# One expert picked from the counts of all but the last tile, its weights asked for ahead of the sort

## The chip, the cores and the metric

The kernel runs on one core of a Trainium2 chip. The metric is the device time of one execution in microseconds; the median of three runs of the kernel before is 2537.41 us.

## The reference, cut to what matters

Two layers, each a token mixer followed by a mixture of experts (MoE). Layer 0 routes 768 tokens (256 context and 512 latent), layer 1 only the 512 latent ones. A router picks a group, and in it the two best of 32 experts for each token; each expert is a gated MLP (1024 to 512 to 1024).

```python
def expert_ffn(xb, e, w_g, w_u, w_d):
    return (jax.nn.silu(xb @ w_g[e]) * (xb @ w_u[e])) @ w_d[e]

def hier_moe(h, w_rg, b_rg, w_re, b_re, w_g, w_u, w_d):
    ...
    flat_e = (grp[:, None] * EXPERTS_PER_GROUP + top_i).reshape(-1).astype(jnp.int32)
    ...
    counts = jnp.zeros((N_EXPERTS,), jnp.int32).at[flat_e].add(1)
    ...
    y = lax.map(lambda a: expert_ffn(a[0], a[1], w_g, w_u, w_d), (xb, blk_e))
    out = jnp.zeros((T + 1, D), F32).at[buf_tok].add(y.reshape(P, D).astype(F32) * buf_w[:, None])
    return out[:T].astype(h.dtype)
```

The weights of an expert are 6 MB (in pieces of 1 MB: four of w_gu, the gate and up matrices together, and two of w_d), and each of the 32 is used in each layer.

## The kernel before

The mixer leaves the tokens as tiles of 128 (six in layer 0, `TL=[0..5]`; four in layer 1, `TL=[2..5]`). A loop over the tiles (L979 to L993) then interleaves the last part of the mixer's output (`mix`) with the router (`norm2`), a generator whose pieces run some rounds later: norm, transposes, router matmuls (L883, result `lgt` on VectorE, L885), the choice of two experts (one-hot rows `OH1`, `OH2`, their sum `M`, L907), positions within an expert (L910 to L912), and the running count `Ms` (L913). The matmuls of this part share one PSUM bank, `ov` (the pool `pso`). At the end of the loop, expert 0's six weight loads are issued.

Behind the loop come loads of the modulation rows `g2` (L1020 to L1027; twelve DMAs in layer 0; nfin and six in layer 1), and the sort (L1084 to L1108): a key of 32 times the count, with a large constant added for the first `NS` experts, whose numbers are known to the program (NS is 1 in layer 0 and 2 in layer 1); a rank from comparisons; and `oi`, the expert number of each rank. The table `SLOTS` gives each rank its number of slots of 32 tokens; what doesn't fit goes to an overflow loop (L1226) that runs as often as is counted in `oi[32]`.

The MoE loop (L1202 to L1218) goes through the ranks: expert 0 (in layer 1, experts 0 and 1), then small and large ranks in turn. For each it reads the expert's number from `oi` into a register of SP (`values_load`, L1203: a TENSOR_LOAD and two short register instructions), issues six loads of 1 MB (`wload`, L959 to L973), gathers the rows of tokens by indirect DMA on GpSimd (L1060), and does the matmuls (L1153 with w_gu, L1178 with w_d). `wload` lets each load wait for the landing of the load four before it. Sixteen buffers of 1 MB are free for weights at the stage's start; the 17th load takes over a buffer of expert 0, once its first products are done.

What sets the order: all these loads, the register loads and the g2 loads are issued by SP, one behind the other, in the order that a scheduler gives when the program is built. Each DMA on SP also waits for the DMA eight before it (eight semaphores in turn). The reload of `br`, the router's bias for layer 1 (L848), is among them: it may overwrite the old one once layer 0's last `lgt` is written.

Of the kernel before, what the change touches and what calls it, by code (L numbers as in the profile page):

```python
# [12 lines left out]
I32 = mybir.dt.int32  # L13
U32 = mybir.dt.uint32
AF = mybir.ActivationFunctionType
OP = mybir.AluOpType
AX = mybir.AxisListType
ET = mybir.EngineType
# [7 lines left out]
NE = 32  # L26
# [1 line left out]
BIG = 4194304.0  # L28
NSL = (1, 2)

SLOTS = ([4, 5, 4, 4, 4] + [3] * 5 + [2] * 18 + [1] * 4, [2, 2] + [3] * 3 + [2] * 11 + [1] * 16)


T1_CA, T1_SA, T1_CR, T1_SR = 0, 512, 1024, 1536
# [27 lines left out]
def tile_backbone(ctx: ExitStack, tc: tile.TileContext, a: dict, out: bass.AP, stop=None, dbg=None):  # L62
    nc = tc.nc
    PE, ACT, DVE, POOL, SP = nc.tensor, nc.scalar, nc.vector, nc.gpsimd, nc.sync
# [19 lines left out]
    def unit(name, dtype=F32, n=2048):  # L84
        return big.tile([128, n], dtype, name=nm(name), tag="c8")
# [16 lines left out]
    def pso():  # L102
        return ps(psov, "ov")

    def small(n, name, dtype=F32, bufs=2):
        return sm.tile([128, n], dtype, name=nm(name), tag=name, bufs=bufs)
# [22 lines left out]
    ident, tri, iota1, iota0, i64 = (cp[:, CP[k][0]:CP[k][1]] for k in ("ident", "tri", "iota1", "iota0", "i64"))  # L129
    tok2, hbm2, zc, bo = (cp[:, CP[k][0]:CP[k][1]] for k in ("tok2", "hbm2", "zc", "bo"))  # L130
# [6 lines left out]
    ones = const(128, "ones")  # L137
# [259 lines left out]
    def layer(l, xt_l, xt_c):  # L397
        full = l == 0
        NS = NSL[l]
        TL = [0, 1, 2, 3, 4, 5] if full else [2, 3, 4, 5]  # L400
# [397 lines left out]
        for bi, b in enumerate("RAF"):  # L798
# [6 lines left out]
            for d in range(8):  # L805
                gp = ahead.pop(0) if ahead else gates(bi, d)
                w = split_load(a["w_br"][l, bi, d]).rearrange("p w (k c) -> p w k c", k=4)
# [45 lines left out]
        Ms = cst.tile([128, NE], F32, name=f"Ms_{l}", tag="Ms_")  # L853
        DVE.memset(Ms, 0.0)

        def norm2(t):
# [29 lines left out]
            g8, gi, gf = small(8, "g8"), small(8, "gi", U32), small(1, "gf")  # L886
# [18 lines left out]
            DVE.tensor_scalar(oh2, iota0, mf[:, 1:2], None, op0=OP.is_equal)  # L905
            M = small(32, "M")
            DVE.tensor_tensor(M, oh1, oh2, op=OP.add)  # L907
            yield
            pp = pso()
            PE.matmul(pp[:, 0:32], tri, M, start=True, stop=False)  # L910
# [19 lines left out]
        def wout(qd):  # L930
            wq = [unit("wqH", R32).rearrange("p (k c) -> p k c", k=8), unit("wqL", R32).rearrange("p (k c) -> p k c", k=8)]
            for k2 in range(4):
                r = raws.tile([128, 512], F32, name=nm("raw"), tag="raw")
                SP.dma_start(r, a["w_out"][l, qd, k2])
                r3 = r.rearrange("p (k c) -> p k c", k=2)
                ks = slice(k2 * 2, k2 * 2 + 2)
                split_to(wq[0][:, ks, :], wq[1][:, ks, :], r3)
            return wq
# [20 lines left out]
        def wload(e, parts=range(6)):  # L959

            res = []
            for j in parts:
                n, j = ("w_gu", j) if j < 4 else ("w_d", j - 4)
                src = a[n][l, e:e + 1] if isinstance(e, int) else a[n][l, bass.ds(e, 1)]
                src = src[0, j // 2] if n == "w_gu" else src[0]
                t = unit(n)
                d = SP.dma_start(t, src[:, (j % 2) * 2048:(j % 2) * 2048 + 2048])
                if len(queue) >= 4:
                    tc.add_manual_dep(d.ins, queue[-4].ins.name, SYNC,
                                      reason="few transfers of weights stand before a gather")  # L970
                queue.append(d)
                res.append(t)
            return res  # L973

        wq2 = [wout(2), wout(3)]
        early = 0
        first = wload(0, range(early))
        g = {}
        for i in range(len(TL) + 2):  # L979
            if i < len(TL):  # L980
                t = TL[i]
                mix(2, wq2[0], t)
                g[i] = norm2(t)
                next(g[i])
                mix(3, wq2[1], t)
                next(g[i])
            if 0 <= i - 1 < len(TL):
                next(g[i - 1])
            if i >= 2:
                next(g[i - 2], None)  # L990
            n = 6 if i == len(TL) - 1 else early
            first += wload(0, range(early, n))
            early = n  # L993
# [4 lines left out]
            return None  # L998


        t0 = TL[0]
        NP = len(TL)
        PR = cst.tile([128, NT, NE], F32, name=f"PR_{l}", tag="wr")
# [5 lines left out]
        oi = cst.tile([128, NE + 8], I32, name=f"oi_{l}", tag="oi_")  # L1009
        xgs = []  # L1010
        for _ in range(3):
            t = hls.tile([128, 2, 512], F32, name=nm("xg"), tag="hl")
            POOL.memset(t, 0.0)
            xgs += [t[:, 0, :], t[:, 1, :]]
        g2u = unit("g2")
        if not full:
            nf = g2u[:, 1024:2048]
            SP.dma_start(nf, bcast_rows(a["nfin"], 1024))
        g2 = {}
        for j, sz in enumerate((64, 32)):  # L1020
            w = sz * 8
# [49 lines left out]
        def prep(r):  # L1071
            n = SLOTS[l][r]
            col = (P1 if r < NS else PR)[:, t0:6, r]
# [7 lines left out]
        scat = []  # L1081


        perm = unit("perm")  # L1084
        pc = pso()
        PE.matmul(pc[0:32, 0:1], Ms, ones[:, 0:1], start=True, stop=True, skip_group_check=True)
        PE.matmul(pc[0:32, 4:36], ones[:, 0:32], Ms, start=True, stop=True, skip_group_check=True)
        kc, kr, gt, rc = perm[0:32, 0:2], perm[0:32, 32:64], perm[0:32, 64:96], perm[0:32, 2:3]
        DVE.tensor_scalar(kc[:, 1:2], tok2[0:32, 0:1], -0.5, 32.0, op0=OP.mult, op1=OP.add)
        DVE.tensor_copy(kr, kcon[0:32, 0, :])  # L1090
        for r in range(NS):
            DVE.tensor_scalar(kr[:, 0:r + 1], kr[:, 0:r + 1], 2.0 ** 20, None, op0=OP.add)
            DVE.tensor_scalar(kc[0:r + 1, 1:2], kc[0:r + 1, 1:2], 2.0 ** 20, None, op0=OP.add)
        DVE.scalar_tensor_tensor(kc[:, 0:1], pc[0:32, 0:1], 32.0, kc[:, 1:2], op0=OP.mult, op1=OP.add)
        DVE.scalar_tensor_tensor(kr, pc[0:32, 4:36], 32.0, kr, op0=OP.mult, op1=OP.add)
        DVE.tensor_scalar(gt, kr, kc[:, 0:1], None, op0=OP.is_gt)
        DVE.tensor_reduce(rc, gt, axis=AX.X, op=OP.add)
        ev, cc = perm[0:32, 3:4], perm[0:32, 4:5]
        DVE.tensor_copy(cc, pc[0:32, 0:1])
        DVE.tensor_scalar(ev, tok2[0:32, 0:1], 0.5, -1.0, op0=OP.mult, op1=OP.add)  # L1100
        rr = perm[0:32, 96:192]
        DVE.tensor_scalar(rr[:, 0:32], iota0[0:32], rc, ev, op0=OP.is_equal, op1=OP.mult)
        DVE.tensor_scalar(rr[:, 32:64], ident[0:32, 0:32], rc, None, op0=OP.mult)
# [88 lines left out]
            scat.append(s)  # L1192


        seq, rest = list(range(NS)), list(range(NS, NE))
        while rest:
            seq.append(rest.pop())
            if rest and len(seq) > NS + 3:
# [1 line left out]
        last, xT = None, None  # L1200
        pre += [prep(r) for r in seq[NS:2]]
        for i, r in enumerate(seq):  # L1202
            e = r if r < NS else nc.values_load(oi[0:1, r:r + 1], engines=[ET.SP], min_val=0, max_val=NE - 1)  # L1203
            w = wload(e) if i else first
            wg, wd = w[:4], w[4:]
            blocks = pre.pop(0)
            if max(2, NS) <= i + 2 < NE:
                pre.append(prep(seq[i + 2]))
            for j, (xg, sz, di, ws) in enumerate(blocks):
                if xT is None:  # L1210
                    xT = take(xg, sz)
                nxt = blocks[j + 1] if j + 1 < len(blocks) else (pre[0][0] if pre else None)
                sg = hidden(xT, sz, wg)
                aT = turn(*last[:2]) if last else None
                xT = take(*nxt[:2]) if nxt else None
                if last:
                    give(aT, *last[1:])
                last = (sg, sz, wd, di, ws)  # L1218
# [7 lines left out]
        with tc.If(left > 0):  # L1226
            with tc.For_i(0, left, 1):
# [13 lines left out]
                w = wload(nc.values_load(oi[0:1, 33:34], engines=[ET.SP], min_val=0, max_val=NE - 1))  # L1241
# [10 lines left out]
                gi, di, ws = slots([hot(pcol[:, ts], 0, 64)], 64, lambda t: vc[:, t, :])  # L1252
# [45 lines left out]
def _consts():  # L1298
# [14 lines left out]
    kc[0] = 31 - np.arange(32)  # L1313
    kc[1], kc[2] = 32 * np.array(SLOTS[0]), 32 * np.array(SLOTS[1])
    put("kcon", kc.reshape(1, 96))
# [153 lines left out]
```

## Time and profile before

| | |
|---|---|
| median of 3 runs | 2537.41 us (2535.14 to 2538.32) |
| the profiled execution, its time | 2536.36 us |
| its span in the profile | 2534.4 us |
| mean TensorE clock granted | 0.942 |
| PE (TensorE) busy | 2259.1 us, 89% |
| DVE (VectorE) busy | 994.0 us, 39% |
| ACT (ScalarE) busy | 568.3 us, 22% |
| POOL (GpSimd) busy | 528.7 us, 21% |
| bytes moved | 595.10 MB, 235 GB/s over the span |

The time is a little longer than the span, since it holds what lies around the first and last instruction. The expert stages are at about 880 to 1390 us (layer 0) and 2010 to 2490 us (layer 1). The busy shares are means over mixer and expert stages, which differ; the stages have to be read one by one.

### The profile page before, as it was taken

How to read it: one execution, taken by the hardware profiler on the slowest of the kernel's cores; microseconds unless marked ns; L12 is line 12 of the kernel's file. 1: busy time of each engine (PE TensorE's matmuls, PEld its weight loads, DVE VectorE, ACT ScalarE, POOL GpSimd, SP SyncE). 2: the span in 40 equal slices, each digit the busy share in tenths (PEclk: the TensorE clock that was granted, in tenths of full speed). 3: DMA queues.
4: the chain of work that ended last, by engine and by line, in shares of the span. 5: the costliest groups of instructions: out<-in, count | busy, mean ns of one | idle time of the engine just before them, and what ended most of it. 6: DMA issues, size and time to landing. Idle time of an engine off the chain costs nothing. (4 is left out here: it accounts for less than half of the span.)

```text
span 2534.4 us, 42281 instructions
## 1 busy us (share of the span) xinstructions
PE 2259.1 (89%) x16557; PEld 1491.6 (59%) x16557; DVE 994.0 (39%) x2939; ACT 568.3 (22%) x1248; POOL 528.7 (21%) x436
## 2 busy tenths in 40 slices
PE   5999999999999799999997599999999778877773
PEld 3788767888889743344432488668888633322221
DVE  5534564424234832333332744654334622111112
ACT  4222354212222210111111432453233200000000
POOL 0223342002223311111110323430122311110111
PEclk9999899999999899999999799999999889888877
DMA  7433201435233699999998512112335799999996
GB/s 275 170 129 130 84 18 37 175 129 192 88 113 109 208 410 418 416 381 417 417 420 365 204 57 71 43 50 63 96 97 195 258 416 417 414 417 406 416 420 254
DMA packets 128700, 595.10 MB, mean 235 GB/s; under 512 B 19653, under 2 KB 20765, under 8 KB 72945
## 3 DMA queue, kind: packets, MB, share of 16 engines
q1 hardware_dynamic: 115472, 562.70, 57.5%
q0 software_dynamic: 12064, 26.26, 2.7%
q10 hardware_dynamic: 960, 3.39, 0.4%
q8 instruction: 132, 2.16, 0.3%
q14 instruction: 72, 0.58, 0.1%
HBM read 578.43 MB, written 26.15 MB: 239 GB/s over the span
## 5 line engine op out<-in xcount | busy, mean ns | idle before, releaser
L1153 PE MATMUL mm<-w_gu,xT 128*32 128x256 f32 (+1 forms) x3424 | 530.1, 533 | 133.0 <-DMA w_gu<-in_w_gu_dram 129.3
L1153 PEld LDWEIGHTS mm<-w_gu,xT 128*32 128x32 f32 (+1 forms) x3424 | 170.5, 132 | 429.5 <-issue 203.4
L276 PE MATMUL mm<-hH,hl 128*128 128x512 f32 x736 | 292.8, 399 | 0.2 <-DVE shuf L317 0.2
L277 PE MATMUL mm<-hL,hl 128*128 128x512 f32 x736 | 290.5, 395 | 0.0
L278 PE MATMUL mm<-hH,hl 128*128 128x512 f32 x736 | 288.9, 393 | 1.2 <-DVE hl L239 1.2
L239 DVE TENSOR_TENSOR hl<-raw,hl 128x512 fp32r<-128x512 f32 x248 | 186.0, 752 | 262.3 <-ACT hl L238 261.7
L1178 PE MATMUL mm<-w_d,aT 128*32 128x256 f32 (+1 forms) x1712 | 243.2, 493 | 4.6 <-DVE aT L1168 3.7
L238 ACT CAST hl<-raw 128x512 fp32r<-128x512 f32 x248 | 153.5, 620 | 373.6 <-PE mm L278 227.1
L1187 POOL DMA_INDIRECT y_d<-y,gd x78 | 78.2, 1003 | 750.1 <-DVE y L1186 386.9
L1158 ACT ACTIVATE act<-mm 128x256 f32<-128x256 f32 (+1 forms) x78 | 26.9, 345 | 895.8 <-PE mm L1153 871.2
L1159 DVE TENSOR_TENSOR act<-act,mm 128x256 f32<-128x256 f32 (+1 forms) x78 | 28.8, 369 | 475.2 <-ACT act L1158 475.1
L1178 PEld LDWEIGHTS mm<-w_d,aT 128*32 128x32 f32 (+1 forms) x1712 | 83.4, 126 | 149.0 <-issue 122.6
L278 PEld LDWEIGHTS mm<-hH,hl 128*128 128x128 f32 x736 | 139.0, 189 | 31.6 <-DVE hl L239 1.6
L276 PEld LDWEIGHTS mm<-hH,hl 128*128 128x128 f32 x736 | 138.7, 189 | 30.2 <-issue 2.1
L277 PEld LDWEIGHTS mm<-hL,hl 128*128 128x128 f32 x736 | 139.1, 189 | 27.2 <-issue 2.0
L276 PE MATMUL mm<-hcH,hl 128*128 128x256 f32 x448 | 129.5, 289 | 1.4 <-DVE shuf L317 0.7
L277 PE MATMUL mm<-hcL,hl 128*128 128x256 f32 x448 | 128.6, 287 | 0.0
L278 PE MATMUL mm<-hcH,hl 128*128 128x256 f32 x448 | 128.3, 286 | 0.0
L1060 POOL DMA_INDIRECT xg<-h_d,gd x78 | 82.0, 1051 | 136.3 <-issue 73.2
L623 POOL TENSOR_SCALAR sa<-sa,sv 128x512 f32<-128x512 f32 (+2 forms) x40 | 72.2, 1806 | 135.4 <-DVE sv L621 74.4
L820 POOL TENSOR_TENSOR yl<-yl,sg 128x512 f32<-128x512 f32 x32 | 53.0, 1655 | 195.5 <-DVE sg L819 195.2
L276 PEld LDWEIGHTS mm<-hcH,hl 128*128 128x128 f32 x448 | 86.3, 193 | 8.8 <-DVE shuf L317 1.6
(401 smaller groups left out, 3761.7 us busy)
## 6 DMA issues: line engine op xcount, KB each, us to landing
w_gu<-in_w_gu_dram SPq DMA_DIRECT2D x256, 1024.0 KB, 10.4
w_d<-in_w_d_dram SPq DMA_DIRECT2D x128, 1024.0 KB, 10.5
raw<-in_w_in_dram SPq DMA_DIRECT2D x200, 256.0 KB, 2.6
wada<-in_w_ada_dram SPq DMA_DIRECT2D x48, 1024.0 KB, 5.1
raw<-in_w_br_dram SPq DMA_DIRECT2D x48, 256.0 KB, 2.6
yb<-y_d SPq DMA_DIRECT2D x10, 1024.0 KB, 10.7
raw<-in_w_out_dram SPq DMA_DIRECT2D x32, 256.0 KB, 2.9
h_d<-hb POOLq DMA_DIRECT2D x10, 512.0 KB, 6.9
```

The source lines that it names most:

```text
L238: ACT.copy(hl[:, 0], r)
L239: DVE.tensor_tensor(hl[:, 1], r, hl[:, 0].bitcast(F32), op=OP.subtract)
L276: PE.matmul(o[:, 0:n], wh, h[kc], start=kc == 0, stop=False)
L277: PE.matmul(o[:, 0:n], wh, lo[kc], start=False, stop=False)
L278: PE.matmul(o[:, 0:n], wl, h[kc], start=False, stop=kc == 7)
L623: POOL.tensor_scalar(S[:, 1, 0:W], S[:, 1, 0:W], den[:, 1:2], None, op0=OP.mult)
L820: POOL.tensor_tensor(y, y, sg, op=OP.add)
L1060: POOL.indirect_dma_start(out=xg, out_offset=None, in_=h2_d[l].rearrange("r (a c) -> (r a) c", c=sz * 8), in_offset=bass.IndirectOffsetOnA ...
L1153: PE.matmul(p1[q * sz:q * sz + sz, 0:n], xT[:, k * sz:k * sz + sz], w[:, q * n:q * n + n], start=k == 0, stop=k == 7, skip_group_check=True)
L1159: DVE.tensor_tensor(sv, sv, pv[:, :, 1, :], op=OP.mult)
L1178: PE.matmul(p2[q * sz:q * sz + sz, 0:n], aT[:, j * 128 + q_ * sz:j * 128 + q_ * sz + sz], w[:, q * n:q * n + n], start=k == 0, stop=k == 3 ...
L1187: s = POOL.indirect_dma_start(out=y_d[l].rearrange("r (a c) -> (r a) c", c=n), out_offset=bass.IndirectOffsetOnAxis(ap=di, axis=0), in_=y, ...
```

## The change

A function `choose(t)` is added. It is called in the tile loop when the last tile but one has its `M` (at i == 4 with the fourth of six tiles in layer 0; at i == 3 with the third of four in layer 1). It sums the counts of `Ms` and of that tile in two matmuls, and takes the expert with the lowest count, the first `NS` left out, in seven VectorE operations (a scaling, a max and its index, two casts and an addition; the index takes two). Its number goes to SP by a `values_load` of `cn`. Right behind it, and ahead of the g2 loads in the program's text, stand all loads of expert 1 (layer 1), and six loads (layer 0) or four (layer 1) of the chosen expert, `few`; layer 1's remaining two follow in the MoE loop. In the sort's key the chosen expert gets 2^19 added, so that it has rank NS; SLOTS gives that rank one slot, and the other ranks move up by one. The sums of SLOTS are as before.

```diff
-SLOTS = ([4, 5, 4, 4, 4] + [3] * 5 + [2] * 18 + [1] * 4, [2, 2] + [3] * 3 + [2] * 11 + [1] * 16)
+
+SLOTS = ([4, 1, 5] + [4] * 3 + [3] * 5 + [2] * 18 + [1] * 3, [2, 2, 1] + [3] * 3 + [2] * 11 + [1] * 15)
...
             DVE.tensor_tensor(M, oh1, oh2, op=OP.add)
+            Mt[t] = M
             yield
...
+        def choose(t):
+
+            pp, ck = pso(), small(32, "ck", bufs=1)
+            PE.matmul(pp[0:32, 0:32], ones[:, 0:32], Ms, start=True, stop=False)
+            PE.matmul(pp[0:32, 0:32], ones[:, 0:32], Mt[t], start=False, stop=True)
+            DVE.tensor_scalar(ck[0:32], pp[0:32, 0:32], -1.0, None, op0=OP.mult)
+            c8, ci, cf, cn = small(8, "g8"), small(8, "gi", U32), small(1, "cf", bufs=1), small(1, "cn", I32, bufs=1)
+            DVE.max(c8[0:32], ck[0:32, NS:32])
+            DVE.max_index(ci[0:32], c8[0:32], ck[0:32, NS:32])
+            DVE.tensor_copy(cf[0:32], ci[0:32, 0:1])
+            DVE.tensor_scalar(cf[0:32], cf[0:32], float(NS), None, op0=OP.add)
+            DVE.tensor_copy(cn[0:32], cf[0:32])
+            return cf[0:32], cn
...
+            if i == (4 if full else 3):
+                cf, cn = choose(TL[i - 1])
...
+        perm, g2u = unit("perm"), unit("g2")
...
-        g2u = unit("g2")
+        few = nc.values_load(cn[0:1, 0:1], engines=[ET.SP], min_val=0, max_val=NE - 1)
+        first = [first] + [wload(e) for e in range(1, NS)] + [wload(few, range(6 if full else 4))]
...
+        ev, cc, bp = perm[0:32, 3:4], perm[0:32, 4:5], perm[0:32, 192:225]
+        DVE.tensor_scalar(ev, tok2[0:32, 0:1], 0.5, -1.0, op0=OP.mult, op1=OP.add)
+        DVE.tensor_scalar(bp[:, 0:32], iota0[0:32], cf, 2.0 ** 19, op0=OP.is_equal, op1=OP.mult)
+        DVE.tensor_scalar(bp[:, 32:33], ev, cf, 2.0 ** 19, op0=OP.is_equal, op1=OP.mult)
+        DVE.tensor_tensor(kr, kr, bp[:, 0:32], op=OP.add)
+        DVE.tensor_tensor(kc[:, 1:2], kc[:, 1:2], bp[:, 32:33], op=OP.add)
...
-        seq, rest = list(range(NS)), list(range(NS, NE))
+        seq, rest = list(range(NS + 1)), list(range(NS + 1, NE))
...
-            e = r if r < NS else nc.values_load(oi[0:1, r:r + 1], engines=[ET.SP], min_val=0, max_val=NE - 1)
-            w = wload(e) if i else first
+            if i == NS:
+                first[i] += wload(few, range(len(first[i]), 6))
+            w = first[i] if i <= NS else wload(nc.values_load(oi[0:1, r:r + 1], engines=[ET.SP], min_val=0, max_val=NE - 1))
```

How the built program's order on SP moves. First the start of layer 0's expert stage. The rows are SP's instructions in turn; `w_gu` and `w_d` are weight loads, `g` the g2 loads, `oi` the sorted numbers, `cn` the chosen one. Before, from expert 0's last w_gu on:

```order
L967 DMA w_gu_7836<-in_w_gu_dram 128x2048
L967 DMA w_d_7838<-in_w_d_dram 128x2048
L967 DMA w_d_7840<-in_w_d_dram 128x2048
L1026 DMA g_1187_7940<-mod_d 64x512 x4
L1026 DMA g_1187_7940<-mod_d 32x256 x8
L848 DMA br_16830<-in_b_r_dram 128x40
L1203 TENSOR_LOAD oi_7933
L1203 ISA x2
L967 ISA
L967 DMA w_gu_8215<-in_w_gu_dram 128x2048
```

With the change, from expert 0's first w_d on; 7966 to 7976 are the chosen expert's six, of which the middle ones are left out:

```order
L969 DMA w_d_7852<-in_w_d_dram 128x2048
L1035 TENSOR_LOAD cn_7701
L1035 ISA x2
L969 DMA w_d_7854<-in_w_d_dram 128x2048
L969 ISA
L969 DMA w_gu_7966<-in_w_gu_dram 128x2048
L849 DMA br_16848<-in_b_r_dram 128x40
...
L969 DMA w_d_7976<-in_w_d_dram 128x2048
L1047 DMA g_1191_7944<-mod_d 64x512 x4
L1047 DMA g_1191_7944<-mod_d 32x256 x8
L1229 TENSOR_LOAD oi_7949
```

The register load of cn now stands between loads 5 and 6, br between loads 7 and 8, and the g2 loads behind load 12 instead of behind load 6.

Second, SP ahead of layer 0's 17th weight load. Before (its 16th load, then the overflow loop's count, then the 17th; the register loads of oi stand in lots of four to seven between loads 10 and 16):

```order
L967 DMA w_gu_8349<-in_w_gu_dram 128x2048
L1225 TENSOR_LOAD oi_7933
L1225 ISA x2
L967 ISA
L967 DMA w_d_8351<-in_w_d_dram 128x2048
```

With the change; at the dots stand 23 more register loads of L1229, like the one shown:

```order
L969 DMA w_gu_8367<-in_w_gu_dram 128x2048
L1229 TENSOR_LOAD oi_7949
L1229 ISA x2
...
L1250 TENSOR_LOAD oi_7949
L1250 ISA x2
L969 ISA
L969 DMA w_d_8369<-in_w_d_dram 128x2048
```

So 25 register loads stand between loads 16 and 17 where one stood. In layer 1 they stand as 8 ahead of load 17, 19 ahead of load 18 and two more ahead of load 19; there, cn's register load stands between loads 7 and 8, and nfin and the g2 loads behind load 16 instead of behind load 6.

## Rows read from the trace of the kernel before

**Rows 1.** The page's slices: GB/s in 40 equal slices of the span.

```profile
GB/s 275 170 129 130 84 18 37 175 129 192 88 113 109 208 410 418 416 381 417 417 420 365 204 57 71 43 50 63 96 97 195 258 416 417 414 417 406 416 420 254
```

**Rows 2.** Stretches: length, busy us (instructions) of PE, PEld, DVE, ACT, POOL, PEclk, DMA share, GB/s.

```profile
862.00:868.00 6.00, 5.28 (x24) 4.62 (x24) 4.59 (x30) 1.74 (x5) 1.85 (x2) 0.58 1.03 349
868.00:880.00 12.00, 6.11 (x63) 5.30 (x62) 10.22 (x55) 0.68 (x3) 0.00 (x0) 0.50 0.18 36
880.00:900.00 20.00, 11.15 (x128) 5.22 (x130) 4.81 (x35) 1.66 (x2) 4.12 (x4) 0.57 1.00 398
...
2002.00:2010.00 8.00, 3.25 (x68) 2.84 (x68) 6.00 (x34) 0.00 (x0) 2.60 (x3) 0.50 0.16 59
```

**Rows 3.** SP's waits, 860 to 990, then 1930 to 2060: total us, times, longest.

```profile
SPq L1203 <- DVE rk L1108: 7.7, 1, 7.7
SPq L1026 <- DMA w_d<-in_w_d_dram: 6.6, 2, 3.4
...
SPq L1203 <- DVE rk L1108: 10.3, 1, 10.3
```

**Rows 4.** Stretches in layer 0; waits of PE (950 to 960) and SP (1100 to 1125).

```profile
940.00:960.00 20.00, 16.87 (x210) 8.16 (x204) 5.40 (x25) 1.06 (x3) 5.07 (x5) 1.00 1.02 415
980.00:1000.00 20.00, 20.00 (x175) 9.24 (x173) 5.61 (x25) 1.16 (x3) 4.08 (x4) 1.00 1.02 418
1100.00:1120.00 20.00, 20.00 (x207) 8.06 (x206) 7.15 (x27) 2.20 (x7) 4.09 (x4) 1.00 0.87 340
...
PE mm L1153 <- DMA w_gu<-in_w_gu_dram: 3.1, 4, 1.6
...
SPq L967 <- PE mm L1178: 10.1, 4, 7.5
```

**Rows 5.** SP's DMA queue (packets, MB, share): 878 to 906, 1942 to 2008, 1942 to 2032.

```profile
q1 hardware_dynamic: 1397, 10.27, 93.6%
...
q1 hardware_dynamic: 1936, 11.40, 48.5%
...
q1 hardware_dynamic: 2924, 18.70, 57.5%
```

**Rows 6.** VectorE's order of time (start, us); last, both starts of L1107.

```profile
856.84 0.18 DVE L907 TENSOR_TENSOR M<-POH 128x32 f32<-128x32 f32 x1
...
868.13 0.20 DVE L885 TENSOR_TENSOR lgt<-ov,br 128x40 f32<-128x40 f32 x1 [1.31 <-PE ov L883]
...
1992.30 0.19 DVE L907 TENSOR_TENSOR M<-POH 128x32 f32<-128x32 f32 x1
...
L1107 DVE CAST oi<-ov x2: 191/191/191, 876.1 to 2002.3; 128x32 int32<-128x32 f32 x2
```

**Rows 7.** SP's DMA issues in order of time: start, length of the lot.

```profile
865.46 2.17 SPq L1026 DMA_DIRECT2D g<-mod_d  x5
868.36 0.35 SPq L848 DMA_DIRECT2D br<-in_b_r_dram  x1
877.68 3.38 SPq L967 DMA_DIRECT2D w_gu<-in_w_gu_dram  x4
```

**Rows 8.** Landing of gathers (layers 0, 1), of 256 KB loads; first L1153, layer 1.

```profile
DMA to landing us min/median/max: 7.5/7.7/7.7
...
DMA to landing us min/median/max: 3.3/3.7/5.9
...
raw<-in_w_in_dram SPq DMA_DIRECT2D x4, 256.0 KB, 2.7
...
2011.28 8.02 PE L1153 MATMUL mm<-w_gu,xT 128*64 128x512 f32 x32 [0.46 <-ACT xT L1143]
```

**Rows 9.** Line L1203, 2002 to 2009.2: duration ns min/median/max, first and last start.

```profile
L1203 SPq TENSOR_LOAD <-oi x11: 264/269/275, 2002.6 to 2008.6; - x11
L1203 SPq FUSED_REGOPS  x11: 147/147/159, 2002.9 to 2009.0; - x11
L1203 SPq SEQ_ASSERT  x11: 18/18/18, 2003.1 to 2009.2; - x11
```

More of the change, by code (lines that the diff above doesn't have):

```diff
@@ L973, in wload @@
             return res
+        def choose(t):
[10 more added lines that the diff above has]
+            return cf[0:32], cn
+        Mt = {}
         wq2 = [wout(2), wout(3)]
@@ L1081, in layer @@
         scat = []
-        perm = unit("perm")
         pc = pso()
@@ L1097, in layer @@
         DVE.tensor_reduce(rc, gt, axis=AX.X, op=OP.add)
-        ev, cc = perm[0:32, 3:4], perm[0:32, 4:5]
         DVE.tensor_copy(cc, pc[0:32, 0:1])
-        DVE.tensor_scalar(ev, tok2[0:32, 0:1], 0.5, -1.0, op0=OP.mult, op1=OP.add)
         rr = perm[0:32, 96:192]
```

## The prediction

> **What bounds the kernel now.** I read the page's slices of DMA traffic first: in slices 14 to 20 and 32 to 38, counted from 0, the engines move 381 to 420 GB/s [rows 1]. These are the two expert stages, in which 32 experts of 6 MB pass through SBUF (192 loads of 1.0486 MB per layer, all issued by SP). At 416 GB/s one load takes 2.52 us. The DMA table by stretches shows the place the change aims at: in layer 0 the share is 1.03 up to 868, 0.18 from 868 to 880 and 1.00 after, in layer 1 it is 0.16 from 2002 to 2010 [rows 2]. That is (1-0.18)*12 = 9.8 us and (1-0.16)*8 = 6.7 us without traffic. The view of waits on SP names the cause: L1203, the register load of the sorted expert numbers, waits 7.7 and 10.3 us for the sort [rows 3], with all further loads behind it.
>
> Is the stream of weights the bound right behind the holes? In layer 1 yes. In layer 0 only half: between 940 and 960 TensorE waits 3.1 us for w_gu, then it is busy all the time (20.00 of 20 us from 980 to 1000), and at 1100 to 1120 DMA falls to 0.87 because SP waits for TensorE to free buffers [rows 4]. So a stream that runs d us **late** at 950 makes all of layer 0 d later, and one that is early gains at most about 3.1 us there; in layer 1 a stream that is early gains up to the 6.7.
>
> **The change part by part.** I number the weight loads of a layer 1, 2, 3 and compare one thing: when the stream, having run dry, starts again, and how many loads have landed then. Before, queue q1 has moved 10.27 MB from 878 to 906 [rows 5]; with the six loads landed earlier the 16th is complete at 10.486 MB, by 0.4 MB per us at **906.6**. In layer 1, q1 has moved 11.40 MB at 2008 (ten loads and 0.91 MB of others) and 18.70 MB at 2032: the 17th is complete at 0.91+17.83 = 18.74 MB, **2032.1**.
>
> *What is removed:* the wait for the sort stands no longer ahead of loads 7 to 12 (layer 0) or ahead of 11 to 16 (layer 1). Its 9.8 and 6.7 us are the most that can come back.
>
> *What is added on SP, and what is queued behind it.* (a) The register load of cn. In layer 0 it stands between loads 5 and 6. M of the fourth tile starts at 856.84 [rows 6]; behind it come two matmuls and seven small VectorE operations of about 0.2 us each, among others; I put cn at 860.5. From a written oi (876.1+0.19) to the first issue behind it SP took 1.4 us (877.68) [rows 6, 7]. So load 6 goes at 861.9 instead of 854, load 7 right behind. The queue still holds loads 4 and 5, so this costs little by itself. In layer 1 it stands between loads 7 and 8: M of TL[2] starts at 1992.30 [rows 6], cn at 1995.0, load 8 at 1996.4.
> (b) The reload of br (layer 0 only) waits for the last tile's lgt, 868.13 before [rows 6]. It now stands ahead of loads 8 to 12 and not behind everything that is free to go. choose lies in the router's chain (seven operations on VectorE, and the only PSUM bank of that pool), some 1.2 us: lgt 869.3, load 8 at 870.0, its traffic 1.0 later (issue 877.68, traffic from 878.65 by the shares).
> (c) The g2 loads. Each DMA of SP waits for the landing of the one eight before it; before, this was a wait of 6.6 us for w_d [rows 3]. Now the eighth of the twelve waits for load 12. Five loads from 871.0 take 12.6 us, the g2 pieces between them about 1.5 (an estimate; layer 1's g2 and nfin are the 0.91 MB above), to 885.1; landing is reported 1.0 later (a 256 KB load takes 2.7 us issue to landing [rows 8], of which 0.63 is data and 1.0 the start). The last four go by 887.6 (five took 2.17 us [rows 7]), then the oi load, so load 13 goes at 889.0.
> (d) The register loads of oi. Their number is about the same, but where they stand is not. Before, 31 lie between loads in lots of 4 to 7; now 25 stand in one block ahead of load 17, and in layer 1 8 and 19 ahead of loads 17 and 18. Eleven started from 2002.6 to 2008.6 [rows 9]: 0.60 us each. In layer 0: loads 13 to 15 until 891.2 (four took 3.38 [rows 7], some 1.1 each), 5 register loads 3.0 and 0.5 for the issue, load 16 at 894.7, 25 register loads 15.0, load 17 at 909.7, traffic **910.7**. By then the queue is empty (16 loads, done at about 899) for some 11 us. 910.7-906.6 = **+4.1 us**.
> In layer 1: eight loads from 1997.4 take 20.2, the last g2 waits for the eighth (load 15) and goes at 2018.6; 8 register loads and the issue of load 17 take 5.4, 2024.1; 19 more 11.4: load 18 at 2035.5, traffic 2036.5 with 17 landed. 2036.5-2032.1 = **+4.4 us**.
>
> Here a page of the skill bears on a choice. Rows 9 give two readings of one register load: its three parts are busy for 0.269+0.147+0.018 = 0.43 us, its pitch is 0.60. I take the pitch, since SP is the engine that counts. The Trainium skill, "DMA: Bandwidth & Descriptors", section "Latency and other measured facts", gives a floor of about 600 ns for a tensor_load; as an estimate by that page the block of 25 is 15.0 us, as by the pitch, and it speaks against the second rival below.
>
> *Edits that I cost at nothing.* The sort's five extra VectorE operations (1.0 us) delay oi, but oi is now read at 887.6 and 2018.6, long after. Expert 0's gathers start some 2 us later; in layer 0 the 3.1 us of [rows 4] hide that. In layer 1 the gathers landed in 3.3 to 5.9 us beside an idle queue and in layer 0 in 7.5 to 7.7 beside weights [rows 8]: TensorE starts expert 0 there not at 2011.28 [rows 8] but about 8 us later (2.8 router, 1.0 sort, 4 gather), at 2019.3, and frees the first of its four w_gu buffers a quarter of 8.02 us on, at 2021.3, still before load 17 can go. Loads and blocks are as many as before, as the slot table is permuted only. By the inputs the chosen experts are 17 (17 tokens) and 10 (13); one slot of 32 holds each, and the overflow loop stays empty.
>
> The sum: 4.1+4.4 = 8.5 us on the profiled execution's 2536.36 (its span is 2534.4): 2544.9, as a round number **2545.0**. The median of the runs shown is 2537.41, so this is 0.3% above it.
>
> *Bounds.* Low: register loads at 0.43 take 4.2 off layer 0 (30 of them) and 3.8 off layer 1 (27), together +0.5. High: landings 1 us later at each of the chains (b) and (c), g2 at twice the time and choose at twice the time add about 3.5 and 2.5, together +14.5 (2551).
>
> **The rivals.** *The holes fill (faster).* The mechanism is the intended one: loads 7 to 12 go in the hole, and SP is through its register loads while they still run. It decides at load 17's traffic before 906.6 and load 18's before 2032.1. For it: 9.8 and 6.7 us are there. Against: br and the landing of load 12 hold SP into the time in which the register loads could have hidden. Were load 8 not held by br, layer 0 would be up to 8 us earlier and gain the 3.1; layer 1 must restart before 2030 to gain 2 to 6. Price: 2526 to 2531.
> *It cancels (no change).* The register loads run at 0.43 in an undisturbed block, or the blocks start 3 us earlier: +0.5 to +4, 2537 to 2541. For it: no row shows a lot of 25. Against: the lot of eleven.
> *TensorE becomes late as well (slower still).* Gathers queue behind six extra loads and expert 0 starts so late that buffers, not SP, hold load 17 on. It decides from a start delay over 3.1+4.1 = 7 us in layer 0, where TensorE has no idle time after 960. Price about 5 more, 2550. Against: the queue is empty when layer 0's gathers go.
> *It does not do what it says:* a wrong or overfull choice would run the overflow loop; the counts exclude it.
>
> **How the numbers follow.** 0.2% (5 us) is about what a measurement of this kernel can tell from no change: 2532.3 to 2542.5. The forecast (2543 to 2549) has 0.53, TensorE late 0.10, cancels 0.24, holes fill 0.13. Slower 0.63, same 0.24, faster 0.13. The range 2531 to 2552 holds the forecast, both bounds and the cancelled case; outside are most of the filled holes and the tail of the late TensorE.
>
> **What would show it.** In the changed profile: load 6's issue near 862, 8 to 12 near 870, right after br; load 17 issued near 910 behind 25 register loads and a hole in DMA of about 11 us before it; load 18 near 2035.5 with a hole before it. The share from 868 to 880 should be about 0.8. If load 17 goes before 905.6, or the pitch in the block is under 0.5, the step (d) is wrong; if TensorE waits for gathers beyond 899 in layer 0, it is the third rival.

## The result, and the profile after

The changed kernel takes 2549.45 us (median of 6 runs, 2545.42 to 2553.84), the kernel before beside it 2536.27 (6 runs): a ratio of 1.0055, interval 1.0045 to 1.0065. It is **slower by 13.2 us**, where 8.5 was forecast; the time lies in the range of 2531 to 2552. The profiled execution of the change took 2550.74 us (span 2548.8), that of before 2536.36 (2534.4).

The page of the changed kernel: busy time of the engines, then the slices of DMA traffic, as [rows 1].

```profile
PE 2275.2 (89%) x16565; PEld 1503.9 (59%) x16565; DVE 994.4 (39%) x2961; ACT 568.8 (22%) x1248; POOL 524.3 (21%) x436
...
GB/s 265 177 129 129 83 18 41 170 149 173 87 112 112 261 336 418 417 379 410 417 419 366 205 59 67 42 54 67 95 101 181 285 370 417 412 417 407 417 420 255
```

Slices 13 and 14, in which layer 0's weights begin to stream, went from 208 and 410 GB/s to 261 and 336; slices 30 to 32, at layer 1's start, from 195, 258 and 416 to 181, 285 and 370. In slices 13 and 31 bytes moved earlier, and in the slice behind each more was lost than had been won; layer 1's slices are also shifted, as that layer begins 8.4 us later. Stretches of the changed kernel (columns as [rows 2], which answers to the first three lines; then layer 0's new hole, and the second hole in layer 1 with the restart behind it):

```profile
862.00:868.00 6.00, 5.39 (x27) 4.87 (x26) 4.07 (x28) 1.74 (x5) 1.95 (x2) 0.57 0.93 296
868.00:880.00 12.00, 6.00 (x62) 5.30 (x62) 10.32 (x60) 0.68 (x3) 0.00 (x0) 0.50 0.94 345
880.00:900.00 20.00, 11.64 (x136) 5.83 (x136) 5.42 (x38) 1.66 (x2) 4.12 (x4) 0.66 0.91 314
...
902.60:913.00 10.40, 10.40 (x62) 3.38 (x59) 2.65 (x6) 1.24 (x3) 0.00 (x0) 1.00 0.02 9
912.00:914.00 2.00, 1.72 (x57) 0.96 (x56) 0.75 (x1) 0.00 (x0) 0.55 (x1) 1.00 0.37 78
...
2036.00:2038.00 2.00, 1.54 (x10) 0.66 (x10) 0.99 (x3) 0.64 (x2) 0.00 (x0) 1.00 0.43 180
2038.00:2040.00 2.00, 2.00 (x12) 0.58 (x8) 0.00 (x0) 0.00 (x0) 0.00 (x0) 1.00 0.00 0
2042.00:2044.00 2.00, 2.00 (x12) 0.72 (x10) 0.67 (x5) 0.00 (x0) 1.00 (x1) 1.00 0.01 0
2044.00:2046.00 2.00, 2.00 (x10) 0.54 (x8) 0.62 (x2) 0.63 (x2) 0.00 (x0) 1.00 0.58 119
2046.00:2048.00 2.00, 2.00 (x12) 0.72 (x10) 0.00 (x0) 0.00 (x0) 0.00 (x0) 1.00 0.93 365
```

The old hole is closed: the DMA share from 868 to 880 rose from 0.18 to 0.94. A new one of 10.4 us stands behind it, from 902.6 to 913, at a share of 0.02. What SP does there is in its order of DMA issues (start, length of the lot), seven lines of layer 0, then four of layer 1:

```profile
861.08 0.35 SPq L969 DMA_DIRECT2D w_gu<-in_w_gu_dram  x1
868.07 0.33 SPq L849 DMA_DIRECT2D br<-in_b_r_dram  x1
868.65 1.60 SPq L969 DMA_DIRECT2D w_gu<-in_w_gu_dram  x3
872.06 4.43 SPq L969 DMA_DIRECT2D w_d<-in_w_d_dram  x2
876.54 13.41 SPq L1047 DMA_DIRECT2D g<-mod_d  x12
890.87 6.75 SPq L969 DMA_DIRECT2D w_gu<-in_w_gu_dram  x4
912.33 0.94 SPq L969 DMA_DIRECT2D w_d<-in_w_d_dram  x2
...
2005.12 4.14 SPq L969 DMA_DIRECT2D w_d<-in_w_d_dram  x2
2011.38 8.19 SPq L969 DMA_DIRECT2D w_gu<-in_w_gu_dram  x4
2020.10 7.66 SPq L1047 DMA_DIRECT2D g<-mod_d  x6
2032.71 11.73 SPq L969 DMA_DIRECT2D w_d<-in_w_d_dram  x2
```

Load 16 is the last of the lot at 890.87 (ended 897.6), load 17 the first at 912.33. No DMA lies between, and the register loads fill the time (line L1229; windows 888 to 913 and 2020 to 2050; the columns are those of [rows 9]):

```profile
L1229 SPq TENSOR_LOAD <-oi x30: 260/266/284, 890.0 to 910.6; - x30
...
L1229 SPq TENSOR_LOAD <-oi x29: 262/267/280, 2027.8 to 2045.0; - x29
```

Of the 30, six lie ahead of load 16; the 25th behind it is that of the overflow loop's count (L1250). The 29 of layer 1 are its 8, 19 and 2. Before, 24 of them lay between 885.2 and 901.1, and from 885 to 901 the DMA share was 1.02 and 417 GB/s came in: they ran while loads were on their way.

```profile
885.00:901.00 16.00, 10.73 (x55) 4.23 (x51) 1.37 (x9) 1.66 (x2) 1.99 (x2) 0.62 1.02 417
```

SP's waits, 850 to 920, then 1980 to 2055 (total, times, longest), as [rows 3]:

```profile
SPq L849 <- DVE g L888: 6.8, 1, 6.8
SPq L1035 <- DVE cn L988: 5.8, 1, 5.8
...
SPq L1035 <- DVE cn L988: 12.9, 1, 12.9
```

The wait for the sort is gone; the one for the choice (`cn`) and the one of `br`, put down to a VectorE result of the router, stand earlier.

**Where the 13 us lie.** To compare all kernels by the same parts, I cut each profiled span at three rows: the first weight load's issue in layer 0, the start of the last w_d product of that layer, and the first weight load's issue in layer 1. For the change these are:

```profile
829.03 0.33 SPq L969 DMA_DIRECT2D w_gu<-in_w_gu_dram  x1
...
1398.87 3.65 PE L1202 MATMUL mm<-w_d,aT 128*64 128x512 f32 x16 [0.81 <-DVE aT L1192]
...
1951.20 0.33 SPq L969 DMA_DIRECT2D w_gu<-in_w_gu_dram  x1
```

so "layer 0" is 1398.87-829.03 = 569.84, "between" (layer 1's mixer) 552.33, and "layer 1" 2548.8-1951.20 = 597.60. Before they are 561.26, 552.34 and 591.64: +8.6 in layer 0, +6.0 in layer 1, nothing between. Here are all profiled executions, with the experiments of the next section (us; ratio and interval from the timed runs):

| kernel | layer 0 | between | layer 1 | ratio to before |
|---|---|---|---|---|
| before | 561.26 | 552.34 | 591.64 | 1 |
| the change | 569.84 | 552.33 | 597.60 | 1.0055 [1.0045, 1.0065] |
| e9, the change again | 568.12 | 555.22 | 598.93 | 1.0048 [1.0034, 1.0062] |
| e1, register loads spread | 561.79 | 554.43 | 586.77 | 0.9988 [0.9978, 0.9999] |
| e2, br later | 566.60 | 552.48 | 597.10 | 1.0055 [1.0038, 1.0072] |
| e10, br later, again | 565.73 | 553.68 | 597.00 | 1.0042 [1.0029, 1.0056] |
| e3, g2 first | 561.59 | 552.13 | 588.10 | 0.9987 [0.9977, 0.9997] |
| e6, e1 to e3 together | 563.88 | 555.50 | 586.51 | 0.9995 [0.9985, 1.0006] |
| e4, choice without early loads | 561.77 | 554.34 | 592.71 | 1.0005 [0.9996, 1.0015] |
| e5, numbers known | 562.95 | 550.47 | 583.86 | 0.9965 [0.9951, 0.9979] |
| e8, layer 1 alone, as it is | 562.45 | 550.33 | 596.82 | 1.0026 [1.0011, 1.0040] |
| e7, layer 1 alone, spread | 564.46 | 552.91 | 585.64 | 0.9985 [0.9975, 0.9995] |
| e12, the same again | 563.56 | 552.59 | 585.74 | 0.9976 [0.9966, 0.9985] |
| e11, chosen expert first | 558.59 | 554.03 | 586.22 | 0.9958 [0.9943, 0.9973] |

One profile doesn't give layer 0 to better than about 1.6 us: the five kernels with layer 0's old order (before, e4, e7, e8, e12) lie between 561.3 and 564.5, mean 562.7. "Between" varies by 5 us among kernels that leave it alone. "Layer 1" falls into clear groups: 596.8 to 598.9 with the block of register loads, 591.6 and 592.7 with the old order, 585.6 to 588.1 with early loads and no block.

### The profile page after: what moved, and what is told of

Its sections match the earlier page's. It is cut to its first block, busy times and chain, and to the rows that moved or that the text cites. A ratio compares the mean times of both kernels' runs of the same rounds, so it can differ in the third digit from the quotient of the medians.

```text
span 2548.8 us, 42317 instructions
## 1 busy us (share of the span) xinstructions
PE 2275.2 (89%) x16565; PEld 1503.9 (59%) x16565; DVE 994.4 (39%) x2961; ACT 568.8 (22%) x1248; POOL 524.3 (21%) x436
## 5 line engine op out<-in xcount | busy, mean ns | idle before, releaser
L1177 PE MATMUL mm<-w_gu,xT 128*32 128x256 f32 (+1 forms) x3424 | 543.3, 540 | 123.4 <-DMA w_gu<-in_w_gu_dram 119.8
L1177 PEld LDWEIGHTS mm<-w_gu,xT 128*32 128x32 f32 (+1 forms) x3424 | 177.4, 133 | 425.7 <-issue 220.4
```

Source lines behind the costliest of these rows:

```text
L1177: PE.matmul(p1[q * sz:q * sz + sz, 0:n], xT[:, k * sz:k * sz + sz], w[:, q * n:q * n + n], start=k == 0, stop=k == 7, skip_group_check=True)
```

## The experiments

**The block or TensorE (e1).** The forecast's theory is that SP, busy with register loads beside an empty queue, costs the time. Rivals: TensorE starts late or has no more to gain; the choice's own work costs it. e1 leaves the change as it is, but each register load may only be issued behind the last load but three (an order, no wait):

```
+ if i > NS:
+     ld, v = nc.values_load_multi_w_load_instructions(oi[0:1, r:r + 1], engines=[ET.SP], min_val=0, max_val=NE - 1)
+     tc.add_manual_dep(ld[0].ins, queue[-4].ins.name, NOSYNC, reason="one register load for one expert")
- w = first[i] if i <= NS else wload(nc.values_load(oi[0:1, r:r + 1], engines=[ET.SP], min_val=0, max_val=NE - 1))
+ w = first[i] if i <= NS else wload(v[0])
```

> The changed kernel with one edit: each register load of oi is held, in SP's order only, behind the weight load four before its own expert's first, so that SP meets one register load per expert and no block of 25 (layer 0) or 8 and 19 (layer 1). Everything else stays. Theory A (the new holes come from SP reading registers while the queue is empty): load 13 still goes at about 891 in layer 0, load 17 goes at about 902 or as soon as expert 0's first products free its buffer, not at 912; in layer 1 load 18 goes some 9 us sooner. Layer 0 loses its 7 to 8 us and gains up to TensorE's 3 us, layer 1 loses its 6 and gains some 4: 2528 to 2534, clearly under both kernels' order of things now (2549) and at or under the kernel before. Theory B (TensorE is late: choose lies in the router's chain and expert 0's gathers stand behind weights, so buffers hold the loads): the holes shift to a wait of SP for L1177, time stays over 2545.

Measured: 2531.6 us (10 runs), 18 less than the change and 0.1% under the kernel before. Layer 1 is 586.8, 10.8 under the change and 4.9 under before; there the stream is whole. Layer 0 is back to 561.8, but no better than before. SP's issues around load 17 tell why, with its waits from 850 to 915 and the stretch from 900 to 910:

```profile
891.81 3.51 SPq L970 DMA_DIRECT2D w_gu<-in_w_gu_dram  x4
905.00 2.05 SPq L970 DMA_DIRECT2D w_d<-in_w_d_dram  x2
```

```profile
SPq L970 <- PE mm L1178: 9.6, 2, 8.0
```

```profile
900.00:910.00 10.00, 9.54 (x46) 3.15 (x44) 1.53 (x4) 0.76 (x2) 0.00 (x0) 1.00 0.75 286
```

Load 17 goes at 905.00, hardly other than before (904.63), and now SP waits 8.0 us for matmuls of L1178: the 17th load takes over a buffer of expert 0, and TensorE gives the first one back only in the second block of that expert's tokens, which begins at 903.02 (TensorE's rows):

```profile
892.58 9.39 PE L1178 MATMUL mm<-w_gu,xT 128*64 128x512 f32 x32 [0.46 <-ACT xT L1168]
903.02 3.65 PE L1178 MATMUL mm<-w_gu,xT 128*64 128x512 f32 x16 [0.46 <-ACT xT L1168]
```

**br's place (e2, e10).** In both, the reload of br may go only behind load 31 of layer 0:

```
- SP.dma_start(br, bcast_rows(a["b_r"][l:l + 1], 40))
+ bd = SP.dma_start(br, bcast_rows(a["b_r"][l:l + 1], 40))
+ if not full:
+     tc.add_manual_dep(bd.ins, late[-1], NOSYNC, reason="behind the first loads of weights")
...
+ late.append(queue[30].ins.name)
```

> The changed kernel with one edit: the reload of br for layer 1 is held, in SP's order only, behind layer 0's 31st weight load, so that loads 8 to 12 no longer stand behind the last tile's router logits. Only layer 0 can move. Theory A: loads 8 to 12 go 5 to 6 us earlier (863 to 866 instead of 868.6 and on), the g2 loads and load 13 follow as much earlier, the block of 25 register loads starts and ends as much earlier, load 17 goes near 906.5 instead of 912.3: 5 to 6 us less than the changed kernel, 2543 to 2545. Theory B: nothing to gain, 2549.

> The changed kernel with br behind load 31 again. In its profile layer 0's loads came 4 to 5 us sooner than in the changed kernel, but its first times (4 runs) were only 2 us less. If br's place costs what the profile shows: 4 to 5 us under the changed kernel beside it, 2544 to 2546. If it costs nothing: within 1 us of it.

2547.41 (4 runs) and 2548.01 (5 runs), against 2549.45 and, in e10's company, 2549.74. The gain is about 2 us, neither the 4 to 6 nor the nothing of the two theories, and its interval reaches to none; layer 0 shows 566.6 and 565.7, 2 to 4 under the change. Counted from each profile's first weight load, load 17 goes at 81.0 and 79.9 us instead of 83.3. br's place is no main cause. The reason is in the traffic: while SP waits for br until 868, loads 4 to 7 are still moving (share 0.93 from 862 to 868, above; from 829 to 868 SP's queue moved 7.09 MB, and loads 1 to 7 are 7.34).

**The g2 loads first (e3).** The early loads move behind the g2 loads, so that the block begins sooner, while loads still run:

```
- few = nc.values_load(cn[0:1, 0:1], engines=[ET.SP], min_val=0, max_val=NE - 1)
- first = [first] + [wload(e) for e in range(1, NS)] + [wload(few, range(6 if full else 4))]
...
+ few = nc.values_load(cn[0:1, 0:1], engines=[ET.SP], min_val=0, max_val=NE - 1)
+ first = [first] + [wload(e) for e in range(1, NS)] + [wload(few, range(6 if full else 4))]
```

> The changed kernel with one edit: the register load of cn and the early loads stand in the text behind the nfin and g2 loads and not ahead of them (as the g2 loads stand in the kernel before). The register loads of oi then start as soon as oi is written and no longer behind the landing of load 12 (layer 0) or 15 (layer 1); they are as many. Theory A: layer 0: load 13 near 880, the lots of 2, 4, 5 and 19 register loads end near 901 instead of 911, load 17 near 902; layer 1: load 18 near 2034 instead of 2044 by the changed kernel's times. The 17th load's restart comes before 906.6 in layer 0 and the 18th's before 2032 of the kernel before in layer 1: 2528 to 2535. Theory B: 2545 or more.

2531.89 (10 runs), as good as e1. Ahead of layer 0's load 17 there are as many register loads as in the change (31), but 12 of them now stand between loads 12 and 16 and the block behind load 16 has 19, not 25; load 13 goes at 884.38 and load 17 at 906.55:

```profile
884.38 10.78 SPq L969 DMA_DIRECT2D w_gu<-in_w_gu_dram  x4
906.55 1.11 SPq L969 DMA_DIRECT2D w_d<-in_w_d_dram  x2
```

A hole is left (share 0.14 from 902 to 904, 0.00 to 906), but by the shares 16 loads have landed at about 902, where the kernel before has them at 906.6. So it isn't the register loads' number that costs, but where they stand and what lies beside them.

**The choice alone (e4).** The choice and the new ranks stay, the early loads go; all register loads come from oi again.

```
- few = nc.values_load(cn[0:1, 0:1], engines=[ET.SP], min_val=0, max_val=NE - 1)
- first = [first] + [wload(e) for e in range(1, NS)] + [wload(few, range(6 if full else 4))]
...
+ e = r if r < NS else nc.values_load(oi[0:1, r:r + 1], engines=[ET.SP], min_val=0, max_val=NE - 1)
+ w = wload(e) if i else first
```

> The changed kernel without the early loads: choose, the changed key, the permuted slot table stay, but the chosen expert's and expert 1's weights are asked for in the MoE loop by oi, as in the kernel before. It prices choose and the sort by themselves. In the changed kernel oi is written 0.6 us later than before in layer 0 (876.7) and, counted from each kernel's first weight load of layer 1, 3.6 us later in layer 1. Theory A: both holes grow by as much, 2536.3+0.6+3.6 = 2540 to 2541, so at most 4 of the change's 13 us come from here. Theory B (the router's delay is the main loss): 2545 or more.

2537.72 (10 runs) against 2536.1: +1.6, interval -1.0 to +3.8 us. The choice and the longer sort cost at most a third of the change's loss, perhaps nothing.

**What the holes can give at most (e5).** The kernel before, with each rank's number fixed in the program, so that no load waits for the sort and there are no register loads but the last count's, which goes behind all weight loads. It leaves out the choice of the right expert for each block.

```
- e = r if r < NS else nc.values_load(oi[0:1, r:r + 1], engines=[ET.SP], min_val=0, max_val=NE - 1)
+ e = r
...
```

> The kernel before with the sort taken out of SP's way altogether: the MoE loop takes expert r for rank r (a number known to the program) and not oi[r], so that no weight load waits for the sort and SP reads no registers between loads. It leaves out the choice of the right expert for each block (loads, gathers and products are as many, with other weights). This is more than the change could ever reach, and so a bound of what the two holes are worth. In the run with spread register loads the 17th load of layer 0 waited 8 us for L1178's products: all 16 buffers were full and the first is given back in expert 0's second block of tokens, near 905, as in the kernel before (904.63). Theory C (buffers, not the stream, bound what an early start can give): layer 0 gains nothing (load 17 at 904 to 905), layer 1 gains only what lies between its own first freed buffer and the old stream, 3 to 6 us: 2530 to 2533. The prediction's account (3.1 us in layer 0, 6.7 in layer 1): 2526 to 2527.

2527.84 (5 runs), 8.3 less than before, all of it in layer 1 (583.9, -7.8). There this is more than theory C's 3 to 6 us and a little more than the 6.7 that the prediction put as the most; for layer 0 theory C holds. Layer 0 gains nothing, even with nothing in SP's way: load 13 goes at 879.67, 11 us sooner than before, load 17 at 904.15. SP's waits, 850 to 960, and then the stretches:

```profile
SPq L968 <- PE mm L1154: 20.6, 4, 11.6
```

```profile
890.00:900.00 10.00, 9.31 (x35) 3.34 (x36) 0.42 (x1) 1.66 (x2) 0.00 (x0) 0.68 0.71 286
900.00:910.00 10.00, 9.25 (x44) 2.78 (x40) 1.45 (x4) 0.82 (x3) 0.00 (x0) 1.00 0.48 156
```

By the shares all 16 buffers are full at about 897, and the hole that was at 868 to 880 is at 897 to 905. It was moved, not filled.

**All three edits (e6).** e1, e2 and e3 in one kernel (their diffs, above).

> The changed kernel with all three edits: one register load for one expert, br behind load 31, g2 ahead of cn. If each edit only removes the same hole (theory A with C): no better than either alone, 2530 to 2533. If the edits add: 2526 or less.

2535.88 (10 runs), above the 2530 to 2533 expected: the gains don't add. Load 17 goes at 905.35, as in e1, since the same buffer holds it, and layer 1 (586.5) is as in e1. It is 4 us slower than e1; the profile puts half of that in layer 0 and a quarter between, both within the scatter of one profile. Why is open.

**Layer 1 alone (e7, e8, e12).** Layer 0 goes back to the old order; e8 keeps the change in layer 1 as it is, e7 and e12 have e1's spread there.

```
+ NF = NS if full else NS + 1
...
- seq, rest = list(range(NS + 1)), list(range(NS + 1, NE))
+ seq, rest = list(range(NF)), list(range(NF, NE))
```

> The change in layer 1 alone (layer 0 as in the kernel before), with one register load for one expert. Theory C: layer 0's early loads are worth nothing, so this is as good as the run with both layers: 2530 to 2533. If layer 0's part brings its 3 us: 2534 to 2535, above the run with both.

> The change in layer 1 alone, with the register loads where the scheduler puts them (8 and 20 ahead of loads 17 and 18). It splits the loss by layer. Theory A by the prediction's terms: layer 1 +4.4, 2541; by the changed kernel's own trace, in which layer 1's loads fall 5.9 us further behind: 2542. If layer 1 is not at a loss by itself: 2536.

> The change in layer 1 alone with one register load for one expert, in five rounds, as a candidate that is faster than both kernels: 2531 to 2534, 2 to 5 us under the kernel before.

e8: 2541.21 (6 runs), 5.1 over before's median (the ratio's interval is 2.8 to 10.1), with layer 1 at 596.8. The change in layer 1 costs some 5 us by itself, and by difference layer 0 some 8 (3 to 10 by that interval). e7 and e12: 2532.82 (10 runs) and 2532.25 (11 runs), as e1. All that e1 gains over before comes from layer 1.

**A small block first (e11).** If expert 0's buffers hold layer 0, a shorter expert ahead of it must free them sooner. The chosen expert's tokens are one block of 32. e11 is e1 with these two exchanged in layer 0:

```
+ if full:
+     seq[0:2] = [1, 0]
+     pre.reverse()
...
- w = first[i] if i <= NS else wload(v[0])
+ w = first[r] if i <= NS else wload(v[0])
```

> The changed kernel with one register load for one expert, and in layer 0 the chosen expert (one block of 32 tokens) done before expert 0 (two blocks of 64), so that TensorE gives back the first of the 16 buffers some 8 to 10 us sooner. It tests theory C directly. If the full buffers hold load 17 in layer 0: its issue moves from 905 to 893 to 898 and DMA has no hole from 890 to 910. TensorE, which from then on is busy nearly all the time, starts as before, so layer 0's end moves by at most its 3 us of waits at 945 to 960: 2528 to 2533 against 2531.6 of the run with spread register loads alone. If load 17 stays at 904 to 906, theory C is wrong.

**2527.12 us** (4 runs, 2526.37 to 2529.16), ratio 0.9958 [0.9943, 0.9973]: the fastest here, 10.9 under the kernel before in its company (2538.01) and 5.1 under e12 there, which has the old order in layer 0. TensorE's first block and SP's load 17 in order of time, then the stretches:

```profile
891.66 5.75 PE L1178 MATMUL mm<-w_gu,xT 128*32 128x256 f32 x64
...
896.17 2.83 SPq L970 DMA_DIRECT2D w_d<-in_w_d_dram  x2
```

```profile
890.00:900.00 10.00, 9.58 (x128) 5.15 (x130) 2.10 (x12) 2.09 (x4) 0.67 (x1) 0.70 0.88 339
900.00:910.00 10.00, 10.00 (x75) 3.87 (x71) 2.59 (x7) 1.16 (x3) 1.54 (x2) 1.00 1.02 421
```

Load 17 goes at 896.17, 8.8 us before e1's, the share from 900 to 910 is 1.02 instead of 0.75, and layer 0 is 558.6, 4.1 under the mean of the old order.

**The change again (e9),** in the company of e10 to e12.

> The changed kernel itself, beside the next two on the same chip, so that the small difference to the run with br behind load 31 can be told. Expected as in the first measurement: 13 us over the kernel before, 2549 to 2550.

2549.74 (5 runs), 11.7 over before.

## Why the prediction was right in direction and short in size

**The mechanism holds.** Register loads in a block beside an empty queue make the change slower. Spreading the block (e1) or starting it earlier (e3) takes some 18 us off the change, in both layers, in e1 with the choice, the sort, the g2 loads and br left in place. In layer 0 the loss also goes with load 17's lateness. Counted from the layer's first weight load, load 17 goes at 75.3 to 75.6 us in the five kernels with the old order, at 79.9 in e10, 81.0 in e2, 81.8 in e9 and 83.3 in the change, and the layer lasts 562.7 (their mean), 565.7, 566.6, 568.1 and 569.8.

The time itself is a weak witness. It lies just above the forecast of 2543 to 2549, inside the range by its high bound (2551), which has g2 at twice its time among its terms, and nearly at the price of the third rival (2550), which is not what happened (below). The holes and the order of SP's issues tell the mechanism, not the number.

**The pitch, step (d), was right.** From the end of load 16's issue (897.62) to load 17 (912.33) lie 14.7 us for 25 register loads, 0.59 each; 0.60 was forecast. The bound of 0.43, and with it the rival that it cancels, falls. The Trainium skill gives a floor of about 600 ns for a tensor_load ("DMA: Bandwidth & Descriptors", "Latency and other measured facts"); the measured 0.59 is near it, though within the block the loads start 0.56 us apart and the row of a TENSOR_LOAD alone shows 0.266.

**Step (c) is the term that was mis-sized in layer 0.** Forecast for the layer +4.1; measured +8.6 in the first pair of profiles, 6.3 as the mean of two profiles of the change (569.0) against five of the old order (562.7), and some 8 by the timed runs of e8 and the change. From load 8 to load 13 the forecast has 19.0 us (870.0 to 889.0); it took 22.2 (868.65 to 890.87). The stretches between show where the 3.2 us went; the last line counts the packets of the last stretch by size:

```profile
868.00:873.00 5.00, 2.54 (x12) 2.14 (x12) 4.29 (x32) 0.68 (x3) 0.00 (x0) 0.50 0.87 247
873.00:884.00 11.00, 4.28 (x96) 3.92 (x96) 9.13 (x50) 0.00 (x0) 0.94 (x1) 0.50 1.00 418
884.00:891.00 7.00, 1.82 (x52) 1.61 (x53) 1.89 (x16) 0.00 (x0) 3.18 (x4) 0.50 0.85 201
DMA packets 938, 1.40 MB, mean 201 GB/s; under 512 B 305, under 2 KB 561, under 8 KB 910
```

At both ends the engines are busy and move little. The weights start slowly, as they do behind other holes (below). The twelve g2 pieces were put at 1.5 us of DMA time between the weights; in the trace they move behind them. From 884 on, 910 of 938 packets are small ones, of g2 and of expert 0's gathers, and the 1.40 MB take 7 us, where 418 GB/s would take 3.4. The eighth piece, which waits for load 12, is issued at 887.72 (886.1 by the forecast). So load 17 came at 912.33 (forecast 909.7) and the traffic at about 913.2 (910.7): 6.6 behind 906.6. The choice itself was not late (lgt's last tile at 867.8, forecast 869.3), so step (c) lost more than load 17 shows, and the earlier start made up for a part.

**Layer 1's chain was right to a microsecond, its price was not complete.** Layer 1 begins 8.44 us later in the change's profile. Load 18's issue ended at 2032.71+11.73 = 2044.4 and began 0.4 earlier, which is 2035.6 on before's clock; forecast 2035.5. By the shares, traffic restarts at 2036.4; forecast 2036.5. Yet the layer costs 5.3 (five profiles with the block, mean 597.5, against 592.2 for the two of the old order), not 4.4. The rest fits what lies behind the restart: from 2044 to 2048 the engines move 119 and then 365 GB/s (above), some 0.8 us less than 418 GB/s from the restart on would be (an estimate from these rows). The forecast let the stream come back at full speed at once. Two more register loads stand ahead of load 19, so load 18 runs alone at first; but the kernel before, without them, starts as slowly behind its hole in layer 0, so how much of the 0.8 is theirs no run tells:

```profile
878.00:880.00 2.00, 1.32 (x26) 1.23 (x24) 2.00 (x8) 0.00 (x0) 0.00 (x0) 0.50 0.68 156
```

**Step (b) was right on br's place and wrong on its price.** br went at 868.07, loads 8 to 10 from 868.65, 1.4 us earlier than forecast. But "up to 8 us earlier" without it, as the rival of the filled holes had it, is not there: 2 us (e2, e10). The forecast counted the time in which SP waits, and not whether the loads ahead were still moving. They were (share 0.93 from 862 to 868), and from 868 to 880 the share came to 0.94, not to the forecast 0.8.

**The rival of the filled holes was wrongly argued for layer 0.** Its price was 3.1 us of TensorE's waiting there plus 2 to 6 in layer 1. Layer 1 gives what it said or a little more: -7.8 in e5, and -6.0 as the mean of the five kernels with the spread. Layer 0 gives nothing (e1, e5), since load 17 must wait for expert 0's first buffer until about 905 in both. For this rival the forecast had looked at the buffers of layer 1 (freed at 2021.3, before load 17) and not at those of layer 0, which it let hold load 17 only in the third rival, where TensorE starts late; TensorE started in time, and they held it all the same. e11 bears it out: with a small block first the buffers come free at 896, and layer 0 is 4 us shorter, in one profile, and 5 by the timed runs beside e12.

**TensorE late fell.** In layer 0 TensorE's first product is at 892.43 (before 892.65), in layer 1 at 2027.36, which is 2018.9 on before's clock, 7.6 later than before; forecast 8.0. e1 has the same choice, sort and gathers and is faster than before; e4 bounds their cost at 1.6 us, +3.8 at the most.

**TensorE's clock stands nowhere in the forecast.** From 940 to 960 TensorE was granted 0.84 of its clock in the change, and 1.00 before [rows 4]: about a third of these 20 us lay on the lower of its two levels (1.2 GHz).

```profile
940.00:960.00 20.00, 15.98 (x220) 8.36 (x222) 6.95 (x31) 1.73 (x5) 5.44 (x6) 0.84 1.02 416
```

At the second of two falls in and near this stretch, close to 955, TensorE was waiting 2.2 us for w_gu. Whether the lower clock cost time no run shows by itself. The change, e9, e2 and e10 were granted 0.85, 0.90, 0.85 and 0.95 from 930 to 965 (before and e1: 1.00), and what layer 0 takes behind load 17 is 486.5, 486.3, 485.6 and 485.8 us, without that order.

## What to carry to other kernels

When an instruction that waits is moved away from a queue, count everything that will now stand in a block where it used to be spread, and ask whether transfers run beside that block: here it was 25 register loads of 0.59 us ahead of one load. Loads that are asked for earlier help only as far as there are buffers for them. Find who gives the next one back, and when, before counting a hole as a gain; where that is a long block of work, putting a short one ahead may be what makes the earlier loads pay.

## What had not been expected of the hardware

Small pieces keep the engines busy and move little: from 884 to 891, with the g2 pieces and expert 0's gathers nearly alone, a DMA share of 0.85 moved 201 GB/s, where a share of 1.00 had moved 418 with weights just before. How much of this is the g2 rows' read of one row for all partitions, how much their size, and how much the gathers, no run here tells apart. And a stream starts slowly behind a hole: a share of 0.58 moved 119 GB/s from 2044 to 2046, 0.37 moved 78 from 912 to 914 and, in the kernel before, 0.68 moved 156 from 878 to 880, in each case about half of what the same share moves later.
